# Attention outputs of tokens from 512 on: stored as two half-precision parts and turned by DMA transposes instead of by TensorE

## The chip, the cores and the metric

The kernel runs on one core of a Trainium2 chip. The time is in device microseconds (us) for one launch. A core has five engines with queues of their own, each working strictly in order: TensorE (PE in the profile, its weight loads PEld) for matmuls, VectorE (DVE) and ScalarE (ACT) for element-wise work, GpSimd (POOL) and SyncE (SP), which in this kernel mainly issue DMAs. An engine waits for another, or for a DMA, on semaphores.

## The reference

One decoder layer over 2048 tokens of width 1024. Two kinds of attention share one normalised input and one input projection; their outputs are gated, put side by side, sent through an output projection, normalised again and added to the input:

```python
oa = forgetting_attention(qa, ka, va, fa + b_fgate)      # 8 heads of 64, causal, decaying
oa = oa * silu(za)
ob = sliding_window_sink_attention(rope(qb), rope(kb), vb, sinks)   # 8 heads of 64, window 128
ob = ob * silu(zb)
y = concatenate([oa, ob], axis=-1) @ w_out
x = x + gate * rms_norm(y, g_post)
```

Everything is float32 in the reference. The kernel computes its large products with float32 numbers split into two float16 parts, high and low, and three matmuls per product (high by high, high by low, low by high).

## The kernel before, in words

The work goes in stages, all of it on one core, in an order that is written out by hand: the code lists small units of TensorE work, and a counter of ticks (`after(n, f)` puts work n ticks off, `tick()` runs what is due) decides when the VectorE and ScalarE work that belongs to a unit is put into the queues. Because queues are in order, the place at which a step is put in is also the place at which it can hold up what follows.

1. Input normalisation and the first projections. The gate inputs z, transposed (width in partitions, tokens along the free side), go to a DRAM tensor `z_d`.
2. Sliding-window attention (class `Pair`): 4 pairs of heads by 8 pairs of 128-query blocks, 32 windows, with projection units (L317, L335) put in between. The last step of a window (`out_`, L911 to L916) multiplies the PSUM result by 1/sum into a float32 tile `on` and GpSimd's queue stores it to the DRAM tensor `o_d`.
3. Forgetting attention (class `Step`): 8 heads, each with four chunks of 512 queries (`ci`) and 20 steps of two key blocks. A step takes scores (L1294 to L1297), exponentials (ScalarE, L1301), their split into parts (ScalarE L1305, VectorE L1308) and products with the values (L1318 to L1321). At the last step of a chunk the result is multiplied by 1/sum into `ona` (L1327), and SP stores it to `o_d` (L1328). Projections of later heads and the search for row maxima (L1245, L1248) stand between the steps. The queries, keys and extra rows of a head live in one of two large SBUF tensors, `Ts[0]` for even heads and `Ts[1]` for odd ones, each of four slots of 2048 half-precision columns.
4. Output (class `Out`), one object for each of 16 tiles of 128 tokens. `load` (L1398) brings the tile's row of `o_d` (tokens in partitions) and its gate z (width in partitions) into slots of `Ts[0]`, which is free since head 7 lives in `Ts[1]`. `turn` (L1406) transposes o with eight 128x128 float32 TensorE transposes into two PSUM banks (L1410). `gate` (L1416 to L1419) multiplies both banks with z on VectorE. `squares_` (ScalarE, L1423) sums squares, `scale_` adds them over partitions with a one-column matmul (L1427) and makes a power-of-two-like scale, and two more steps split the scaled product into high (ScalarE, L1437) and low (VectorE, L1438). `product` (L1489) multiplies with the output weights: 16 units per tile, each of three matmuls 128x512, in two halves of eight units; at the end of a half `evac` (L1498, L1499) reads the bank. `root` and `store` normalise, add x and write the result (L1518, L1519).

The units of stage 4 stand in a list `ounits`, about 16 per tile. The first 33 of them are spread over the last twelve steps of head 7; the others follow after the last step, two units to a tick. In this list, a tile's load stands two tiles ahead of its products, and its turn stands in the first half of the tile before it. Every SP transfer also waits for an older one: SP's DMAs share eight semaphores in turn.

Of the kernel before, what the change touches and what calls it, by code (L numbers as in the profile page):

```python
# [10 lines left out]
F32 = mybir.dt.float32  # L11
# [30 lines left out]
def hybrid_layer(  # L42
# [794 lines left out]
    class Pair:  # L837
# [62 lines left out]
        def pv(self):  # L900
            j, i = self.j, self.i
            po = ps_pv.tile([P, 4, 64], F32, tag="pv", name="pob")
            for e, (i_, k0, nk) in enumerate(self.blocks):
                for h in range(2):
                    for b in range(nk):
                        for n, (pp_, vv) in enumerate(((0, 0), (0, 1), (1, 0))):
                            PE.matmul(po[:, 2 * e + h, :], self.ptt[:, pp_, self.at[e] + h * nk + b, :],  # L907
                                      vb[:, k0 + b, self.g, 64 * vv:64 * vv + 64],
                                      start=(b == 0 and n == 0), stop=(b == nk - 1 and n == 2))

            def out_():  # L911
                on = onp.tile([P, 2, P], F32, tag="on", name="on")
                V.tensor_tensor(on[:].rearrange("p e (h d) -> p (e h) d", h=2), po[:],
                                self.rinv[:].unsqueeze(2).broadcast_to([P, 4, 64]), op=ALU.mult)
                G.dma_start(o_d[i // 4][(i % 4) * P:(i % 4 + 2) * P, (4 + j) * P:(5 + j) * P]
                            .rearrange("(e p) c -> p e c", p=P), on[:])  # L916

            after(1, out_)

# [356 lines left out]
    class Step:  # L1276
# [33 lines left out]
        def pv(self):  # L1310
            hd, ph = self.hd, self.ph
            if self.first:
                self.po_[0] = ps_po.tile([P, 4, 65], F32, tag="po", name="poa")
            po = self.po_[0]
            for n, (b, u0, o) in enumerate(self.blocks):
                for u in range(u0, 4):
                    pq = slice(o + (u - u0) * P, o + (u - u0 + 1) * P)
                    PE.matmul(po[:, u, :], ph[:, 0, pq], vt[:, b, hd, 0:65],  # L1318
                              start=(self.first and n == 0 and u == 0), stop=False)
                    PE.matmul(po[:, u, 0:64], ph[:, 0, pq], vt[:, b, hd, 65:VW], start=False, stop=False)  # L1320
                    PE.matmul(po[:, u, :], ph[:, 1, pq], vt[:, b, hd, 0:65], start=False,  # L1321
                              stop=(self.last and n == len(self.blocks) - 1))
            if self.last:
                rinv = sm(4, "a_ri")
                V.reciprocal(rinv[:], po[:, :, 64])
                on = op_.tile([P, 4, 64], F32, tag="ona", name="ona")
                V.tensor_tensor(on[:], po[:, :, 0:64], rinv[:].unsqueeze(2).broadcast_to([P, 4, 64]), op=ALU.mult)  # L1327
                SP.dma_start(o_d[self.ci][:, hd * 64:(hd + 1) * 64].rearrange("(u p) d -> p u d", p=P), on[:])  # L1328

        po_ = {}  # L1330

# [38 lines left out]
    w_raw = {}  # L1370

    def w_out_load(m):
        k, cc = m % KT, slice((m // KT) * CH, (m // KT + 1) * CH)
# [18 lines left out]
    class Out:  # L1392
# [5 lines left out]
        def load(self):  # L1398
            t = self.t
            rows_ = slice(t * P, (t + 1) * P)  # L1400
            self.o = Ts[0][:, t % 2, :].bitcast(F32)
            SP.dma_start(self.o, o_d[t // 4][(t % 4) * P:(t % 4 + 1) * P, :])
            self.z = Ts[0][:, 2 + t % 2, :].bitcast(F32).rearrange("p (k n) -> p k n", k=KT)
            SP.dma_start(self.z, z_d[:, :, rows_].rearrange("k p n -> p k n"))

        def turn(self, lag):  # L1406

            px = [bk[bank()][:].rearrange("p (k n) -> p k n", k=4) for _ in range(2)]
            for k in range(KT):
                PE.transpose(px[k // 4][:, k % 4, :], self.o[:, k * P:(k + 1) * P], ident[:])  # L1410
            self.hl = wpool.tile([P, 2, KT, P], F16, tag=("whl", "wraw")[self.t % 2], name="oz")
            self.sc = sm(1, "w_pw")
            hi, lo = self.hl[:, 0], self.hl[:, 1]
            gs = sm(1, "w_mx")

            def gate():  # L1416
                for h in range(2):
                    z = self.z[:, 4 * h:4 * h + 4, :]
                    V.tensor_tensor(z, px[h], z, op=ALU.mult)  # L1419

            def squares_():
                junk = stp.tile([P, KT, P], BF16, tag="st", name="zj")
                A.activation(junk[:], self.z, AF.Square, accum_out=gs[:])  # L1423

            def scale_():
                pg = bk[bank()][:, 0:1]
                PE.matmul(pg, ones[:], gs[:], start=True, stop=True)  # L1427
# [92 lines left out]

    outs = [Out(t) for t in range(NB)]

    ounits, oloads = [], {}
    for t, n in [(0, 0), (1, 0), (0, 1), (1, 1)] + [(t, n) for t in range(2, NB) for n in range(2)]:
        if n == 0 and t + 2 < NB:
            oloads[len(ounits)] = t + 2
        for q in range(KT):
            ounits.append(lambda t=t, n=n, q=q: outs[t].product(n, q))
            nxt = 2 if (t, n) == (0, 1) else t + 1 if n == 0 and 2 <= t < NB - 1 else None
            if q == 2 and nxt:  # L1530
                ounits.append(lambda nxt=nxt: outs[nxt].turn(4))
    opos = [0]
    N_IN = 4 * KT + 1

    def ofill(n, each=None):
        for _ in range(n):
            if opos[0] in oloads:
                outs[oloads[opos[0]]].load()
            ounits[opos[0]]()
            opos[0] += 1  # L1540
            if each:
                each()

    with tc.manual_schedule():
# [30 lines left out]
        for s, stp_ in enumerate(steps):  # L1575
# [43 lines left out]
            if not opened and pos[0] >= N_OPEN and (r >= 14 or not late):  # L1619
# [22 lines left out]
        tick()  # L1642
        tick()
        fxs.close()
        ofill(len(ounits) - opos[0], tick2)
        for _ in range(4):
            tick()

    foxo.close()
    fox.close()  # L1650
    bkx.close()
# [30 lines left out]
```

## Time and profile before

| what | value |
|---|---|
| median of 3 runs | 1189.14 us (1188.18 to 1190.87) |
| span of the profiled execution | 1188.7 us |
| what the page shows of that execution beside its span | nothing |
| instructions on TensorE, matmuls and weight loads each | 10853 |
| output transposes on TensorE (L1410) | 128, from 975.6 to 1161.8 us |
| last scores of head 7 | 1016.94 us |
| DRAM traffic | 71.04 MB read, 25.18 MB written |

In the profile a group's row reads: line, engine, operation, output and inputs by the program's names, shape, count, then busy time in us and mean duration in ns, then the idle time of the engine just before these instructions and what ended it. The chain is followed back from the last instruction, at each step to what released it. In the rows by stage, each engine's busy time is followed by its instruction count, in the order TensorE, its weight loads, VectorE, ScalarE, GpSimd; then come the granted TensorE clock, the share of time that the DMA engines are busy, and GB/s.

### The profile page before, as it was taken

The numbers are of one execution on the slowest core, as the hardware profiler recorded it, in microseconds if no ns is written. First come the engines' busy times: TensorE is split into PE (matmuls) and PEld (weight loads), VectorE is DVE, ScalarE is ACT, GpSimd is POOL, SyncE is SP. The second block draws the span as 40 slices with busy tenths as digits, with TensorE's granted clock in tenths as the row PEclk, the third lists the DMA queues.
The fourth block names the chain that finished last, engine by engine and source line by source line (L and its number), as shares of the span: only waits on it lengthen the run. The fifth ranks groups of instructions, "written<-read, shape, count | busy, mean of one in ns | idle before, by whom it ended". The sixth has DMA issues, their size and how long they took to land.

```text
span 1188.7 us, 27244 instructions
## 1 busy us (share of the span) xinstructions
PE 1147.3 (97%) x10853; PEld 693.6 (58%) x10853; DVE 914.1 (77%) x2263; ACT 665.9 (56%) x1102; POOL 115.2 (10%) x231
## 2 busy tenths in 40 slices
PE   5899999999999998999999999999999999999997
PEld 2475556765558976555555555555555555555554
DVE  7876678687776748688888889887888887766665
ACT  2784345464655521476766667666666778433332
POOL 2000112212121211001000101001000000000000
PEclk9899999999999999999999999999999999999999
DMA  9745433314223322413325322212311345455642
GB/s 333 277 121 87 84 89 99 61 59 109 83 70 88 58 63 63 65 50 95 68 70 72 102 63 60 50 48 71 48 42 39 92 127 176 147 171 184 198 167 96
DMA packets 87579, 120.22 MB, mean 101 GB/s; under 512 B 27508, under 2 KB 63388, under 8 KB 87452
## 3 DMA queue, kind: packets, MB, share of 16 engines
q1 hardware_dynamic: 76184, 85.69, 24.4%
q0 software_dynamic: 10832, 32.50, 13.2%
q8 instruction: 85, 1.39, 0.6%
q14 instruction: 42, 0.34, 0.1%
q10 hardware_dynamic: 436, 0.28, 0.1%
HBM read 71.04 MB, written 25.18 MB: 81 GB/s over the span
## 4 chain that ended last, share of the span: by engine, by line
PE 79%; DVE 10%; DMA 6%; issue 2%; ACT 2%; SPq 1%; DVEq 0%; ACTq 0%
PE bk L317 29%; PE bk L1489 13%; PE bk L335 7%; PE sta L1295 4%; PE sta L1294 4%; PE bk L1245 4%; PE poa L1320 2%; PE poa L1321 2%; PE poa L1318 2%; DMA wa<-in_w_ada_dram 2%; PE pxb L888 2%; PE pss L855 2%; PE pob L907 2%; DVE a_m L1248 1%; PE bk L1410 1%
## 5 line engine op out<-in xcount | busy, mean ns | idle before, releaser
L1301 ACT ACTIVATE p<-sta,lift,scl_qk 128x1024 f32<-128x1024 f32 (+2 forms) x160 | 172.0, 1075 | 143.7 <-PE sta L1295 88.2
L317 PE MATMUL bk<-hT,wh_qk 128*128 128x512 f16 x768 | 195.3, 380 | 0.0
L1248 DVE TENSOR_REDUCE a_m<-bk 128x1 f32<-128x512 f32 x192 | 130.5, 686 | 55.2 <-PE bk L1245 54.0
L1308 DVE TENSOR_TENSOR pha<-p,pha 128x1024 f16<-128x1024 f32 (+2 forms) x160 | 169.1, 1057 | 0.2 <-ACT pha L1305 0.2
L1489 PE MATMUL bk<-wohl,oz 128*128 128x512 f16 x744 | 167.0, 379 | 0.7 <-DVE oz L1438 0.7
L1305 ACT ACTIVATE pha<-p 128x1024 f16<-128x1024 f32 (+2 forms) x160 | 148.1, 926 | 5.4 <-PE poa L1321 0.7
L1489 PEld LDWEIGHTS <-oz 128*128 128x128 f16 x744 | 71.9, 99 | 79.4 <-DVE oz L1438 2.8
L317 PEld LDWEIGHTS <-wh_qk 128*128 128x128 f16 x768 | 72.5, 98 | 78.2 <-issue 6.6
L1321 PE MATMUL poa<-vt,pha 128*128 128x65 f16 x1088 | 116.1, 192 | 1.4 <-DVE pha L1308 1.2
L1318 PE MATMUL poa<-vt,pha 128*128 128x65 f16 x1088 | 116.5, 193 | 0.5 <-DVE ona L1327 0.4
L1320 PE MATMUL poa<-vt,pha 128*128 128x64 f16 x1088 | 116.5, 194 | 0.0
L1245 PE MATMUL bk<-T 66*128 66x512 f16 (+2 forms) x320 | 110.2, 350 | 3.1 <-DVE a_m L1248 3.0
L1294 PE MATMUL sta<-T 128*128 128x512 f16 (+1 forms) x320 | 110.9, 346 | 2.5 <-ACT p L1301 2.4
L1318 PEld LDWEIGHTS <-pha 128*128 128x128 f16 x1088 | 101.5, 96 | 15.1 <-DVE ona L1327 1.5
L1295 PE MATMUL sta<-T 69*128 69x512 f16 (+1 forms) x320 | 109.8, 348 | 0.0
L1320 PEld LDWEIGHTS <-pha 128*128 128x128 f16 x1088 | 100.9, 97 | 11.4
L1321 PEld LDWEIGHTS <-pha 128*128 128x128 f16 x1088 | 100.8, 99 | 1.8 <-DVE pha L1308 1.7
L317 PE MATMUL bk<-hT,wh_za 128*128 128x512 f16 x384 | 99.7, 378 | 0.0
L335 PE MATMUL bk<-wh_va,hT 128*128 128x128 f16 x1536 | 90.7, 219 | 0.0
L335 PEld LDWEIGHTS <-hT 128*128 128x128 f16 x1536 | 87.5, 98 | 4.7 <-issue 2.1
L317 PE MATMUL bk<-hT,wh_zb 128*128 128x512 f16 x384 | 88.9, 379 | 0.0
L317 PE MATMUL bk<-hT,wh_qb 128*128 128x512 f16 x384 | 87.4, 379 | 0.0
(498 smaller groups left out, 1860.4 us busy)
## 6 DMA issues: line engine op xcount, KB each, us to landing
hT<-in_x_dram SPq DMA_DIRECT2D x20, 512.0 KB
wa<-in_w_ada_dram SPq DMA_DIRECT2D x16, 512.0 KB
z_d<-tz POOLq DMA_DIRECT2D x32, 256.0 KB, 2.9
T<-stq SPq DMA_DIRECT2D x64, 128.0 KB
T<-o_d SPq DMA_DIRECT2D x16, 512.0 KB
T<-z_d SPq DMA_DIRECT2D x16, 512.0 KB
out_dram<-hT SPq DMA_DIRECT2D x15, 512.0 KB
xt<-in_x_dram SPq DMA_DIRECT2D x12, 512.0 KB
```

The lines of the kernel that those rows point to most:

```text
L317: PE.matmul(ps, whl[:, a, k, :], hT[ci][:, b, k, :], start=(k == 0 and n == 0), stop=(k == KT - 1 and n == 2))
L335: PE.matmul(ps[:, u * P:(u + 1) * P], hT[ci][:, a, k, u * P:(u + 1) * P], whl[:, b, k, :], start=(k == 0 and n == 0), stop=(k == KT - 1 an ...
L1245: PE.matmul(mx[:, :w], T[0:XM, 0, i * P:(i + 1) * P], T[0:XM, 2, pc * CH:pc * CH + w], start=True, stop=True)
L1294: PE.matmul(self.st[:, o:o + w], T[:, 3, kb_], T[:, 1, qc], start=True, stop=False)
L1295: PE.matmul(self.st[:, o:o + w], T[0:XR, 2, kb_], T[0:XR, 0, qc], start=False, stop=not diag)
L1301: A.activation(self.p32[:, :self.w], self.st[:, :self.w], AF.Exp, scale=scl[f"qk{self.hd}"][:], bias=lift[:])
L1305: A.activation(self.ph[:, 0, :self.w], self.p32[:, :self.w], AF.Copy)
L1308: V.tensor_tensor(self.ph[:, 1, :self.w], self.p32[:, :self.w], self.ph[:, 0, :self.w], op=ALU.subtract)
L1318: PE.matmul(po[:, u, :], ph[:, 0, pq], vt[:, b, hd, 0:65], start=(self.first and n == 0 and u == 0), stop=False)
L1320: PE.matmul(po[:, u, 0:64], ph[:, 0, pq], vt[:, b, hd, 65:VW], start=False, stop=False)
L1321: PE.matmul(po[:, u, :], ph[:, 1, pq], vt[:, b, hd, 0:65], start=False, stop=(self.last and n == len(self.blocks) - 1))
L1489: PE.matmul(py, self.hl[:, i, k, :], w_slot(8 * j + k)[:, cc], start=(k == 0 and m_ == 0), stop=(k == KT - 1 and m_ == 2))
```

## The change

Tokens 0 to 511 (tiles 0 to 3) stay as they were. For tokens from 512 on:

- `o_d` holds float16, two parts for each tile. At the end of a window or a chunk the float32 result is no longer stored directly: ScalarE copies it into the high part of a new tile `oh`, VectorE subtracts to get the low part a tick later, and then the same queue as before (GpSimd or SP) stores both parts with one DMA.
- `Out.load` has two DMA transposes, issued by SP, bring the high and the low part from DRAM into SBUF already turned.
- `Out.turn` has no TensorE transposes; `gate` adds both parts into a float32 tile `of` and multiplies that by z, both on VectorE.
- Loads stand four tiles ahead instead of two, in slots of both `Ts[0]` and `Ts[1]`. Tiles 4 and 5 use `Ts[1]`, and their loads are issued in the step before the last one, behind the last scores. Turns stand 22 units ahead of the tile's first product, with one tick more between the gate and the sum.
- A pool for `of` (two buffers of 4 KB per partition) takes the place of the exponentials' tiles, and the scratch for GpSimd's DMA descriptors is set to 8192 bytes per partition.

The diff, cut to its core:

```diff
-    o_d = [dram.tile([CH, D], F32, name=f"o_d{t}") for t in range(NCH)]
+    o_d = [dram.tile([CH, D], F32, name="o_d0")] + [dram.tile([4, 2, P, D], F16, name=f"o_d{t}") for t in range(1, NCH)]
...
+    def o_store(on, pool, ci, rows_, cols_, eng, lag):
+        if ci == 0:
+            eng.dma_start(o_d[0][rows_, cols_].rearrange("(u p) c -> p u c", p=P), on)
+            return
+        u0, u1 = rows_.start // P, rows_.stop // P
+        oh = pool.tile([P, u1 - u0, 2, on.shape[-1]], F16, tag="oh", name="oh")
+
+        def low():
+            V.tensor_tensor(oh[:, :, 1], on, oh[:, :, 0], op=ALU.subtract)
+            eng.dma_start(o_d[ci][u0:u1, :, :, cols_].rearrange("u n p c -> p (u n) c"),
+                          oh[:].rearrange("p u n c -> p (u n) c"))
+
+        after(lag, lambda: A.activation(oh[:, :, 0], on, AF.Copy))
+        after(lag + 1, low)
...
-                G.dma_start(o_d[i // 4][(i % 4) * P:(i % 4 + 2) * P, (4 + j) * P:(5 + j) * P]
-                            .rearrange("(e p) c -> p e c", p=P), on[:])
+                o_store(on[:], onp, i // 4, slice((i % 4) * P, (i % 4 + 2) * P), slice((4 + j) * P, (5 + j) * P), G, 1)
...
-                SP.dma_start(o_d[self.ci][:, hd * 64:(hd + 1) * 64].rearrange("(u p) d -> p u d", p=P), on[:])
+                o_store(on[:], op_, self.ci, slice(0, CH), slice(hd * 64, (hd + 1) * 64), SP, 1 if hd == 7 else 2)
...
         def load(self):
...
+            n = t % 2 if t < 4 or t % 4 > 1 else 2 + t % 2
+            T, n = Ts[n // 2], n % 2
...
+            if t < 4:
+                self.o = o.bitcast(F32)
+                SP.dma_start(self.o, o_d[0][rows_, :])
+            else:
+                self.oT = o.rearrange("p (l k n) -> p l k n", l=2, k=KT)
+                for n in range(2):
+                    SP.dma_start_transpose(self.oT[:, n], o_d[t // 4][t % 4, n])
...
             def gate():
-                for h in range(2):
-                    z = self.z[:, 4 * h:4 * h + 4, :]
-                    V.tensor_tensor(z, px[h], z, op=ALU.mult)
+                if self.t < 4:
...
+                of = ozp.tile([P, KT, P], F32, tag="of", name="of")
+                V.tensor_tensor(of[:], self.oT[:, 0], self.oT[:, 1], op=ALU.add)
+                V.tensor_tensor(self.z, of[:], self.z, op=ALU.mult)
...
-        if n == 0 and t + 2 < NB:
-            oloads[len(ounits)] = t + 2
...
+    for t in range(4, NB):
+        if t > 5:
+            oev.setdefault(start_[t - 4] + 1, []).append(outs[t].load)
+        oev.setdefault(start_[t] - 22, []).append(lambda t=t: outs[t].turn(5))
...
+            if s == len(steps) - 2:
+                outs[4].load()
+                outs[5].load()
...
+        ozp = ozx.enter_context(tc.tile_pool(name="ozp", bufs=2, side="right", reuse_waits="tile"))
...
-    nc = _bacc.Bacc("TRN2", target_bir_lowering=False, num_devices=1)
+    nc = _bacc.Bacc("TRN2", target_bir_lowering=False, num_devices=1, dynamic_dma_scratch_size=8192)
```

More of the change, by code (lines that the diff above doesn't have):

```diff
@@ L1368, in open_out @@
         V.tensor_scalar(wsc[:], fac8[:], ysc[:], None, op0=ALU.mult)
-    w_raw = {}
+    w_raw, ozp = {}, None
     def w_out_load(m):
@@ L1416, in gate @@
             def gate():
-                for h in range(2):
-                    z = self.z[:, 4 * h:4 * h + 4, :]
-                    V.tensor_tensor(z, px[h], z, op=ALU.mult)
+                if self.t < 4:
+                    for h in range(2):
+                        z = self.z[:, 4 * h:4 * h + 4, :]
+                        V.tensor_tensor(z, px[h], z, op=ALU.mult)
+                    return
+                of = ozp.tile([P, KT, P], F32, tag="of", name="of")
+                V.tensor_tensor(of[:], self.oT[:, 0], self.oT[:, 1], op=ALU.add)
+                V.tensor_tensor(self.z, of[:], self.z, op=ALU.mult)
             def squares_():
@@ L1521, in hybrid_layer @@
     outs = [Out(t) for t in range(NB)]
-    ounits, oloads = [], {}
+    ounits, oev, start_ = [], {}, {}
     for t, n in [(0, 0), (1, 0), (0, 1), (1, 1)] + [(t, n) for t in range(2, NB) for n in range(2)]:
-        if n == 0 and t + 2 < NB:
-            oloads[len(ounits)] = t + 2
+        start_.setdefault(t, len(ounits))
         for q in range(KT):
             ounits.append(lambda t=t, n=n, q=q: outs[t].product(n, q))
-            nxt = 2 if (t, n) == (0, 1) else t + 1 if n == 0 and 2 <= t < NB - 1 else None
+            nxt = {(0, 1): 2, (2, 0): 3}.get((t, n))
             if q == 2 and nxt:
                 ounits.append(lambda nxt=nxt: outs[nxt].turn(4))
+    N_IN = 4 * KT + 1
+    oev[0], oev[KT] = [outs[2].load], [outs[3].load]
+    for t in range(4, NB):
+        if t > 5:
+            oev.setdefault(start_[t - 4] + 1, []).append(outs[t].load)
+        oev.setdefault(start_[t] - 22, []).append(lambda t=t: outs[t].turn(5))
     opos = [0]
-    N_IN = 4 * KT + 1
     def ofill(n, each=None):
         for _ in range(n):
-            if opos[0] in oloads:
-                outs[oloads[opos[0]]].load()
+            for f in oev.pop(opos[0], []):
+                f()
             ounits[opos[0]]()
@@ L1647, in hybrid_layer @@
             tick()
+    ozx.close()
     foxo.close()
```

15 lines of the change are left out of this document (9 added, 6 removed).

## Prediction

> **What bounds the kernel now.** I read the page first (span, busy shares, shares of the chain), then busy time by stage, then the chain of waits inside the output stage, where the transposes stand.
>
> ```profile
> span 1188.7 us, 27244 instructions
> ...
> PE 1147.3 (97%) x10853; PEld 693.6 (58%) x10853; DVE 914.1 (77%) x2263; ACT 665.9 (56%) x1102; POOL 115.2 (10%) x231
> ...
> PE 79%; DVE 10%; DMA 6%; issue 2%; ACT 2%; SPq 1%; DVEq 0%; ACTq 0%
> ```
>
> TensorE is on the chain for 79% of the span and VectorE for 10%. By stage (sliding-window attention, the forgetting attention of heads 0 to 6 and part of 7, its last steps, the output products), with DVE and ACT as third and fourth pair of numbers:
>
> ```profile
> 150.00:435.00 285.00, 284.75 (x3330) 199.08 (x3329) 208.44 (x594) 152.27 (x418) 61.74 (x139) 1.00 0.33 78
> 480.00:975.00 495.00, 489.86 (x5020) 283.27 (x5019) 422.26 (x923) 334.12 (x391) 35.10 (x56) 1.00 0.30 66
> 975.00:1018.00 43.00, 41.57 (x448) 25.51 (x445) 32.55 (x57) 38.26 (x50) 0.54 (x1) 1.00 0.51 163
> 1018.00:1166.20 148.20, 147.59 (x800) 76.51 (x799) 97.57 (x275) 48.03 (x89) 0.00 (x0) 1.00 0.54 179
> ```
>
> VectorE is busy 73%, 85%, 76% and 66% of the four; ScalarE 53%, 67%, 89% and 32%. The granted clock (the 1.00) is full. TensorE's busy time has modelled ends, so the chain is the better witness:
>
> ```profile
> by line: PE bk L1489 89.8%; PE bk L1410 7.8%; PE bk L1427 0.9%; DVE hT L1498 0.5%; PE poa L1321 0.3%; DVE pha L1308 0.3%; PE poa L1318 0.2%; PE poa L1320 0.2%; issue 0.0%
> ```
>
> That is 1020 to 1166 us: almost nothing but TensorE, and its transposes (L1410) are 7.8%. A stretch of the same chain:
>
> ```profile
> 1065.80 4.53 PE bk L1489 x21
> 1070.33 0.87 PE bk L1410 x8
> 1071.20 3.88 PE bk L1489 x18
> 1075.09 0.12 PE bk L1427 x2
> ```
>
> Eight transposes are one tile's turn and cost 0.87 us with nothing beside them. A product matmul takes 4.53/21 = 0.216 us, a unit of three 0.65, a tile's 48 matmuls 10.4. With turn and sum a tile takes 11.4 us.
>
> **The change part by part.**
>
> *Removed: the turns of tiles 4 to 15.* By the instruction order this is the only thing that leaves TensorE: 12 x 8 transposes; twelve one-column sums (L1427) only move. 12 x 0.87 = **10.4 us off the path**, and a tile's period falls to 10.5 us. What is late next there is VectorE's gate, below.
>
> *Changed: the gate on VectorE.*
>
> ```profile
> L1419 DVE TENSOR_TENSOR T<-bk,T 128x512 f32<-128x512 f32 x32 | 20.6, 686 | 21.6 <-PE bk L1410 21.6
> ...
> L1308 DVE TENSOR_TENSOR pha<-p,pha 128x1024 f16<-128x1024 f32 x96 | 116.8, 1217 | 0.2 <-ACT pha L1305 0.2
> ...
> L1518 DVE SCALAR_TENSOR_TENSOR hT<-hT,y_rs 128x1024 f32<-128x1024 f32 x15 | 19.1, 1273 | 0.0
> ```
>
> Two multiplications of 0.69 us become an addition of the two parts and a multiplication over 1024 columns. The nearest rows say 1.22 and 1.27 us, so 2.5 instead of 1.4 per tile: +1.1. VectorE works 97.57/148.20 of the stage, 7.5 us a tile; with this 8.6 of 10.5. That is 82%, and TensorE's ten microseconds of products a tile hide it: nothing on the path. Were that cover gone, it would cost at most 12 x 1.1 = 13 us.
>
> *Added: 24 DMA transposes, 256 KB each, on SP's queue.* The trace of before has none, so the price is bounded by its transfers. One tile's 11.4 us in the output stage (the DMA view from 1086.5 to 1097.9), and from the page a transfer of the same size:
>
> ```profile
> q1 hardware_dynamic: 1472, 2.10, 55.8%
> ...
> T<-o_d SPq DMA_DIRECT2D x1, 512.0 KB
> ```
>
> ```profile
> z_d<-tz POOLq DMA_DIRECT2D x32, 256.0 KB, 2.9
> ```
>
> Four transfers of 512 KB fill the engines for 0.558 x 11.4 = 6.4 us. By bytes the load of o is a quarter of that, 1.6 us, and half of it, 0.8 us, is the low end for one transpose. The high end: each of its eight 128x128 blocks takes a whole landing like the 2.9 us, one after another, 23 us. I take 2.9 us, landing and all, from the row with the same bytes.
>
> How much may it cost? In the order, two transposes and a load of z for tile t are issued four tiles ahead, and the gate comes 22 units (14 us) before the tile's products. So latency is covered; rate is not. The other three transfers keep 6.4 - 1.6 = 4.8 us a tile, and of 10.5 us 5.7 are left: **2.85 us of engine time per transpose** is the point from which it would set the pace. A landing of 2.9 us has issue and flight in it, so its engine time is below that. Cost taken: nothing, narrowly.
>
> The start has its own deadline. The first transposes wait for the last scores, whose operands lie where they write:
>
> ```profile
> 1016.94 0.22 PE L1297 MATMUL sta<-dmaskT,identb 128*128 128x128 bf16 x1
> ...
> 1017.19 0.67 ACT L1301 ACTIVATE p<-sta,lift,scl_qk 128x384 f32<-128x384 f32 x1
> ```
>
> From about 1017 us. The products go on at about 1018 with unit 33; tile 4's turn is at unit 44 and its gate a tick later, 1018 + 13 x 0.65 = 1026.5. That is 9.5 us for two transposes and z; at 2.9 us each in a row, 8.7. VectorE now waits there for DMAs. Behind the waiting gate in its order stand the evacuations (L1498) that free TensorE's banks, and TensorE waits for those only when its five banks, each filled for 8 units or 5.2 us, are used up; and the low part of tile 4, planned for unit 58 and needed at 66, has 5.2 us of slack. So nothing is charged unless a transpose takes over some 4.5 us.
>
> *Added: 48 splits of attention outputs.* A ScalarE copy and a VectorE subtraction of 128x256, 24 in each attention.
>
> ```profile
> L1327 DVE TENSOR_TENSOR ona<-poa,a_ri 128x256 f32<-128x256 f32 x32 | 13.6, 424 | 1.1
> ...
> L1126 ACT ACTIVATE wsq<-wsq 128x256 f32<-128x256 f32 x31 | 12.5, 404 | 4.9 <-DMA wsq<-in_w_out_dram 4.9
> ```
>
> 0.42 us on VectorE, 0.40 on ScalarE: 20 us and 19 us of work. What of it reaches the path depends on whether VectorE is behind when it comes. Mostly it isn't; at a head's end it is:
>
> ```profile
> 619.49 0.23 PE bk L1245
> ...
> 619.74 0.69 DVE a_m L1248
> 620.43 1.19 DVE gacc L1182
> ...
> 623.73 0.70 DVE a_m L1248
> ...
> 624.47 0.27 PE bk L1245
> ```
>
> Here TensorE waits 4.7 us for a VectorE backlog, and anything added ahead of it adds its full length. The bounds are none (all in VectorE's idle time) and all of VectorE's 20 us. My choices: a tenth in the sliding-window stage, where VectorE idles 27% (24 x 0.42 x 0.1 = 1.0); a quarter in the 21 splits of heads 0 to 6, where it idles 15% (21 x 0.42 x 0.25 = 2.2); half of both engines' parts for the two splits from 975 to 1018, where ScalarE is 89% busy (2 x 0.82 x 0.5 = 0.8). The last falls after 1018 and costs nothing. Together **4.0 us**.
>
> *Moved: the stores.* They are issued two or three ticks later, from the same queues.
>
> ```profile
> SPq L1328 <- DVE ona L1327: 134.2, 27, 21.2
> ...
> POOL o_d L915 <- DVE on L913: 58.1, 21, 10.0
> ```
>
> Both queues already stand waiting for the store's data, so a later place in line costs them nothing; on SP the store lets short row loads (T<-rw) pass and, late, loads of weights and x; on POOL two small copies. The pieces get smaller (128 bytes on SP instead of 256), with the DMA engines at 0.30 busy. Nothing; a queue held 0.8 us longer before a q/k load (T<-stq) would be the loss, inside the upper bound above. The smaller descriptor scratch of POOL has no row here; its cover is POOL's 10%, and I charge nothing.
>
> *Sum.* The profiled execution's own time is its span of 1188.7 us; the page shows nothing around it. 1188.7 - 10.4 + 4.0 = 1182.3. The median of the runs, 1189.14, lies 0.4 above the span: **1182.7 us**.
>
> **The rivals.**
>
> *Transposes set the pace (slower).* The mechanism is the engines' time per tile: 4.8 + 2c against 10.5 us, for twelve tiles. It decides from c = 2.85 us. At 3.8 us: 12 x 1.9 = 23, so 1206. At 5 us: 52, so 1234. At the 23 us end: 12 x 40.3 = 484, so about 1670. For it: the price taken is close to the point, and no row shows a transfer that turns data. Against it: the row of 2.9 us is a landing, not occupancy; low end 0.8.
>
> [...]
>
> *The splits land where VectorE is behind.* If all of VectorE's 20.2 us reach the path: 1189.1 - 10.4 + 20.2 = 1198.9. The gain is gone at 10.4/20.2, about half. For it: 85% busy and backlogs like the one above. Against: three quarters of the chain is TensorE's.
>
> *The change doesn't do what it says.* The transposes leave, but TensorE stands for the same 0.87 us waiting for low parts, since VectorE's chain per tile got longer: 1189.1 + 4.0 = 1193.1. Against: 8.6 of 10.5 us.
>
> **How the numbers follow.** A run can tell about 0.2% (2.4 us) from no change. Forecast 0.64; transposes set the pace 0.22; splits 0.10; not what it says 0.04. The forecast's own range is 1178 (no cost of the splits, rounded down) to 1187. The range of 8 in 10 runs from 1177 to 1206: it takes in all of the splits' bound and transposes up to 3.8 us; the slower ones (0.16) and a time below (0.03) are left out. Faster by over 0.2% (below 1186.8): the forecast, 0.64. Within: part of the splits' case and of the last, 0.07. Slower: 0.29.
>
> **What would show it.** In the output stage the chain should be L1489's counterpart with no transposes and tile periods of 10.5 us; if transposes set the pace, the periods are uneven or longer, the DMA share is near 1 and VectorE's addition waits on DMA. The first gate should come near 1026 us less what came earlier. In 480 to 975 the stage should grow by about 2 us; 5 or more, and the splits were underpriced. Any wait of the addition on a transpose makes the prediction wrong.

## The result and the profile after

| | before | after |
|---|---|---|
| median (range, runs) | 1189.74 us (1188.18 to 1190.87, 4) | 1184.59 us (1183.7 to 1185.43, 4) |
| profiled execution | span 1188.7 | 1184.12 us, span 1182.4 |

The ratio is 0.9958, with a 95% interval of 0.9944 to 0.9972: faster by 0.42%, 5 us. A later, longer comparison of the same two kernels gave 0.9961 (0.9948 to 0.9973, 12 runs of the changed one). The forecast was 1182.7 us. In spans it was 1182.3, and 1182.4 was measured; that closeness hides errors that cancel, and the sections below take them apart.

The page of the changed kernel, busy times and shares of the chain:

```profile
PE 1136.7 (96%) x10757; PEld 682.6 (58%) x10757; DVE 941.3 (80%) x2311; ACT 680.9 (58%) x1150; POOL 116.1 (10%) x231
...
PE 80%; DVE 10%; DMA 5%; issue 2%; ACT 2%; SPq 1%; DVEq 0%; ACTq 0%
```

TensorE lost exactly 96 matmuls (12 tiles of 8 transposes) and 10.6 us of busy time. VectorE gained 27 us and ScalarE 15 us, and the shares of the chain are nearly unchanged.

To see where the 6.3 us of span went, a stage is best bounded by an operation that both kernels have. The view of one tile gives for each line its durations (min/median/max, ns) and the start of the first and the last of the count. Three such lines cut the span: the last step of a window (`on`), the last step of a chunk (`ona`), and the sum of squares that follows a tile's products (`y_ss`). Before:

```profile
L913 DVE TENSOR_TENSOR on<-pob,b_ri x32: 414/425/426, 165.2 to 433.2; 128x256 f32<-128x256 f32 x32
...
L1327 DVE TENSOR_TENSOR ona<-poa,a_ri x32: 424/424/426, 501.0 to 1023.2; 128x256 f32<-128x256 f32 x32
...
L1509 DVE TENSOR_TENSOR y_ss<-y_ss x15: 150/150/159, 1016.6 to 1172.4; 128x1 f32<-128x1 f32 x15
```

After:

```profile
L928 DVE TENSOR_TENSOR on<-pob,b_ri x32: 410/424/425, 165.4 to 436.4; 128x256 f32<-128x256 f32 x32
...
L1341 DVE TENSOR_TENSOR ona<-poa,a_ri x32: 423/424/426, 503.1 to 1026.5; 128x256 f32<-128x256 f32 x32
...
L1540 DVE TENSOR_TENSOR y_ss<-y_ss x15: 150/152/159, 1020.0 to 1165.8; 128x1 f32<-128x1 f32 x15
```

| stage | before | after | difference |
|---|---|---|---|
| to the first window's result | 165.2 | 165.4 | +0.2 |
| windows (sliding-window attention) | 268.0 | 271.0 | **+3.0** |
| last window to first chunk | 67.8 | 66.7 | -1.1 |
| chunks (heads 0 to 7) | 522.2 | 523.4 | **+1.2** |
| last chunk to first sum of squares | -6.6 | -6.5 | +0.1 |
| output, 14 tile periods | 155.8 | 145.8 | **-10.0** |
| last sum of squares to the end | 16.3 | 16.6 | +0.3 |

The differences add up to -6.3. So the gain is where it was forecast and nearly of the forecast size, and in this pair of profiles a loss of 3.4 us lies ahead of it. By an estimate that is some 1.7 us too little, because the granted clock of the two differed in the third stage of the table (0.91 before and 1.00 after from 470 to 490 us; e8 and e12, below).

The output stage by its chain, 1060 to 1095 us (start, length, what):

```profile
by line: PE bk L1520 99.5%; PE bk L1458 1.3%
...
1061.11 0.12 PE bk L1458 x2
1061.23 10.38 PE bk L1520 x48
1071.61 0.12 PE bk L1458 x2
```

Between a tile's two one-column sums (L1458) stand its 48 products without a break, and the period is 10.5 us; the 0.87 us of L1410 are gone and nothing has taken their place. The gate, by groups:

```profile
L1450 DVE TENSOR_TENSOR T<-of,T 128x1024 f32<-128x1024 f32 x12 | 14.7, 1224 | 0.4
L1449 DVE TENSOR_TENSOR of<-T 128x1024 f32<-128x1024 f16 x12 | 14.6, 1214 | 0.0
```

The addition (L1449) has no idle time before it: in twelve tiles VectorE never waited for a transpose. By stretches, from the start of tile 3's turn to the first product of the last half, first before and then after (TensorE, its loads, VectorE, ScalarE, GpSimd, clock, DMA share, GB/s):

```profile
1024.69:1175.74 151.05, 151.05 (x771) 77.17 (x770) 99.22 (x285) 49.34 (x91) 0.00 (x0) 1.00 0.55 182
```

```profile
1028.07:1169.15 141.08, 141.00 (x674) 66.16 (x673) 111.98 (x286) 49.99 (x91) 0.00 (x0) 1.00 0.68 184
```

VectorE's 12.8 us more lie under TensorE's products (111.98 of 141.08, 79%), and the DMA engines go from 0.55 to 0.68.

### The profile page after: what moved, and what is told of

It reads as the page before. It is cut to its first block, busy times and chain, and to the rows that moved or that the text cites. A ratio compares the mean times of both kernels' runs of the same rounds, so it can differ in the third digit from the quotient of the medians.

```text
span 1182.4 us, 27200 instructions
## 1 busy us (share of the span) xinstructions
PE 1136.7 (96%) x10757; PEld 682.6 (58%) x10757; DVE 941.3 (80%) x2311; ACT 680.9 (58%) x1150; POOL 116.1 (10%) x231
## 3 DMA queue, kind: packets, MB, share of 16 engines
q0 software_dynamic: 10832, 32.50, 13.5%
HBM read 64.75 MB, written 25.18 MB: 76 GB/s over the span
## 4 chain that ended last, share of the span: by engine, by line
PE 80%; DVE 10%; DMA 5%; issue 2%; ACT 2%; SPq 1%; DVEq 0%; ACTq 0%
PE bk L332 31%; PE bk L1520 13%; PE bk L350 7%; PE sta L1309 4%; PE sta L1308 4%; PE bk L1259 4%; PE poa L1334 3%; PE poa L1335 3%; PE poa L1332 3%; DMA wa<-in_w_ada_dram 2%; PE pxb L903 2%; PE pss L870 2%; PE pob L922 2%; DVE a_m L1262 1%; DVE pha L1322 1%
## 5 line engine op out<-in xcount | busy, mean ns | idle before, releaser
L1315 ACT ACTIVATE p<-sta,lift,scl_qk 128x1024 f32<-128x1024 f32 (+2 forms) x160 | 172.0, 1075 | 134.7 <-PE sta L1309 83.9
```

Source lines behind the costliest of these rows:

```text
L1315: A.activation(self.p32[:, :self.w], self.st[:, :self.w], AF.Exp, scale=scl[f"qk{self.hd}"][:], bias=lift[:])
```

## The experiments

The theory at this point: the gain is TensorE's own 12 x 0.87 us; transposes and gate are hidden; the splits cost the heads about 1 us and the windows something. The rivals: the gain comes from elsewhere (loads four tiles ahead, the order of turns); the transposes do cost; the loss in the windows is the splits', the stores', the scratch's, or mere scatter. Each kernel was timed beside the kernel before; the two profiles of one kernel can differ by some us of span (1182.4 and 1185.0 us for the change), so ratios decide on totals and the lines above on stages.

| kernel | median us (runs) | ratio to before [95%] | windows | chunks | output |
|---|---|---|---|---|---|
| before, first profile | 1189.74 (4) | | 268.0 | 522.2 | 155.8 |
| the change | 1184.59 (4) | 0.9958 [0.9944, 0.9972] | 271.0 | 523.4 | 145.8 |
| e1 splits only | 1192.09 (12) | 1.0023 [1.0014, 1.0033] | 270.4 | 523.5 | 156.0 |
| e2 plain copies | 1183.05 (6) | 0.9948 [0.9934, 0.9961] | 270.1 | 523.5 | 145.8 |
| e3 transposes twice | 1207.76 (4) | 1.0152 [1.0135, 1.0169] | 270.9 | 523.6 | 172.0 |
| e4 low part on GpSimd | 1182.86 (6) | 0.9945 [0.9932, 0.9957] | 269.8 | 522.8 | 146.0 |
| e5 no split | 1183.26 (6) | 0.9945 [0.9927, 0.9962] | 271.6 | 522.2 | 145.5 |
| e6 scratch only | 1189.5 (12) | 1.0001 [0.999, 1.0012] | 268.0 | 522.2 | 155.8 |
| e7 turn on TensorE again | 1215.97 (4) | 1.0223 [1.0204, 1.0243] | 270.3 | 523.5 | 177.7 |
| e8 the change again | 1184.34 (12) | 0.9961 [0.9948, 0.9973] | 272.0 | 523.5 | 145.8 |
| e9 idle transposes | 1194.43 (8) | 1.0042 [1.0027, 1.0057] | 269.9 | 523.5 | 156.0 |
| e10 high part only | 1182.95 (6) | 0.9942 [0.9923, 0.9961] | 269.1 | 522.4 | 145.6 |
| e11 split on GpSimd | 1183.21 (6) | 0.9944 [0.9927, 0.9961] | 270.1 | 523.5 | 145.7 |
| e12 before, second profile | 1190.39 (1) | | 268.0 | 522.2 | 155.7 |

The last three columns are worked out from the three lines as in the table above.

**e9: give TensorE its work back, and nothing else.** The change, with eight transposes per tile that nobody reads, at the turn's place:

```diff
+            else:
+                px = [bk[bank()][:].rearrange("p (k n) -> p k n", k=4) for _ in range(2)]
+                for k in range(KT):
+                    PE.transpose(px[k // 4][:, k % 4, :], gacc[:, k * P:(k + 1) * P], ident[:])
```

> The changed kernel with eight TensorE transposes per tile put back where the turn of tiles 4 to 15 stands, on data that has long been there (the gate weights); nobody reads their results. Theory (the gain of the change is TensorE's 12 x 0.87 us, nothing of it was or would be hidden): 10.4 us over the changed kernel, 1194.8, tile periods of 11.4 us. Rival (the output stage waits elsewhere too and hides part of them): 3 to 8 us over it.

Its sum of squares and its chain from 1060 to 1095 us:

```profile
L1544 DVE TENSOR_TENSOR y_ss<-y_ss x15: 150/153/159, 1023.4 to 1179.4; 128x1 f32<-128x1 f32 x15
```

```profile
1060.11 0.87 PE bk L1440 x8
1060.98 5.83 PE bk L1524 x27
1066.81 0.12 PE bk L1462 x2
1066.92 4.55 PE bk L1524 x21
1071.48 0.87 PE bk L1440 x8
```

The output stage takes 156.0 us, that of before, and the median rises to 1194.43, 9.8 above the changed kernel's first median and 10.1 above its second. With loads, order, DMA transposes and gate of the change all in place, the eight transposes alone carry the gain. It also prices the rest of the change: this kernel has all of it without the gain, and is 0.42% (0.27 to 0.57) above before, 5 us. So the result is -10 and +5.

**e2: transposes replaced by plain copies** (the turning is left out):

```diff
-                    SP.dma_start_transpose(self.oT[:, n], o_d[t // 4][t % 4, n])
+                    SP.dma_start(self.oT[:, n], o_d[t // 4][t % 4, n].rearrange("p (k n) -> p k n", k=KT))
```

> The changed kernel, with each DMA transpose replaced by a plain DMA copy of the same 256 KB into the same place, so that the output is computed from unturned data: the turning is left out. Theory (the transposes are hidden, deadline and rate both met): within 0.5 us of the changed kernel, 1184.6. Rival (transposes still cost something on the path, at the first tiles or by SP's time, whose issues of 1.2 to 3.4 us become some 0.4): 1 to 3 us faster, 1182 to 1183.5.

```profile
L1540 DVE TENSOR_TENSOR y_ss<-y_ss x15: 151/153/160, 1017.5 to 1163.3; 128x1 f32<-128x1 f32 x15
```

The output stage is 145.8 us, to the tenth that of the change: turning the data costs the path nothing. The median is 1.5 us lower, which is what the rival said. But the intervals overlap, and the profile has the difference in stages before the first transpose, where the two kernels are alike.

**e3: every transpose issued twice.**

```diff
-                for n in range(2):
+                for n in (0, 1, 0, 1):
```

> The changed kernel with every DMA transpose issued twice into the same place, 48 instead of 24, the result being the same. Theory by DMA engine time: the share of 67.5% in the changed kernel's output stage, less 4.8 us a tile for the other transfers, leaves 2.3 us for two transposes, so four make 4.8 + 4.6 = 9.4 us of a 10.5 us period: within 1 us of the changed kernel, 1184.6. Rival (SP's issue of a transpose, 1.24 to 3.4 us in the trace, is the real price): four issues of about 2 us and three others of 0.5 are 9.5 to 14 us a tile, so up to 12 x 3.5 = 42 us slower, 1190 to 1227.

The expectation that a second set would be hidden too fell: +23 us. The DMA engines from 1060 to 1150 us (packets, MB, share of the 16 engines), and SP's queue:

```profile
q1 hardware_dynamic: 39054, 19.04, 91.2%
...
T<-o_d SPq DMA_TRANSPOSE x29
```

```profile
1106.03 0.53 SPq L1429 DMA_DIRECT2D T<-z_d  x1
1106.61 0.57 SPq L1517 DMA_DIRECT2D hT<-in_x_dram  x1
1107.27 0.38 SPq L1550 DMA_DIRECT2D out_dram<-hT  x1
1107.75 10.06 SPq L1427 DMA_TRANSPOSE T<-o_d  x4
```

The same view of the DMA engines from 1060 to 1123 us, six tile periods, for the change and for e2:

```profile
q1 hardware_dynamic: 20640, 12.59, 74.7%
...
T<-o_d SPq DMA_TRANSPOSE x12
```

```profile
q1 hardware_dynamic: 9677, 12.55, 59.6%
...
T<-o_d SPq DMA_DIRECT2D x12, 256.0 KB
```

From these rows comes the number that the prediction had to bound. In the change the engines are busy for 0.747 x 63 = 47.1 us in six tile periods, 7.8 of each 10.5. Eighteen other transfers at 1.6 us each, by the prediction's row, leave 18.3 us for 12 transposes, 1.5 each. In e2, 0.596 x 63 = 37.5 us leave 8.7 for 12 copies, 0.7 each. These are estimates, since a transfer at a window's edge counts whole or not at all. The packets of the traces can be counted too: only the transposes move packets of 256 bytes, 1024 for each, and only e2's copies packets of 2048. In the same windows a transpose takes **1.4 us** of the engines by this count, a copy 0.7, and a transpose of e3 1.6.

In e3 four transposes at 1.6 and 4.8 us of other transfers are 11.2 us of engine time a tile, more than the 10.5 of the change's period. SP's queue is as full: 10.06 + 0.53 + 0.57 + 0.38 = 11.5 us for one tile's issues. Which of the two holds the stage up wasn't separated: an issue of a transpose took 1.2 to 4.7 us here, and how much of a long one is itself a wait for the engines isn't shown. But waits for DMAs are on the path: of the chain from 1040 to 1150 us, 21.4% are waits for the transposes and 20.3% for the stores of results.

The output stage grew by 26.2 us, and not all of that can be put down to the DMAs. The granted clock, 1.00 in the change from 1028 to 1169 us, was 0.5 in e3 for 27.2 us of the stage, in four stretches from 1038 to 1151 us. One of them, by stretch and in the chain:

```profile
1106.20:1113.00 6.80, 6.11 (x16) 2.52 (x17) 4.90 (x18) 2.45 (x5) 0.00 (x0) 0.50 0.96 270
```

```profile
1107.47 13.19 PE bk L1520 x48
```

Forty-eight products that take 10.38 us at the full clock took 13.19, 2.8 us more for the 5.5 us that they ran at half of it. Had TensorE set the pace in all 27.2 us, the clock would have cost 13.6, an estimate from above. So transposes can bring waits for DMAs onto the path, as the prediction's first rival says, and by engine time the change has a factor of two in hand at most (an estimate: 5.7 us a tile for transposes that take 2 x 1.4); how much of the 26.2 us is the transfers' and how much the clock's stays open.

**e7: the two parts loaded plainly, added on VectorE and turned on TensorE again**, a tick later:

```diff
+            if self.t >= 4:
+                of = ozp.tile([P, KT, P], F32, tag="of", name="of")
+                V.tensor_tensor(of[:], self.oT[:, 0], self.oT[:, 1], op=ALU.add)
...
-            if self.t < 4:
...
+            if self.t < 4:
+                flip()
+            else:
+                after(1, flip)
```

> The changed kernel with the turns of tiles 4 to 15 back on TensorE: both parts loaded by plain copies, added by VectorE, transposed by TensorE a tick later, the gate a tick after that. Theory (the gain is TensorE's 12 x 0.87 us and nothing else): 10.4 us over the changed kernel, 1195, tile periods of 11.4 us. Rival (TensorE had idle time that would have hidden part of the transposes, the gain is the earlier loads): at most 1190.

Measured 1215.97, far above that. Its chain from 1030 to 1150 us:

```profile
1048.62 1.23 DVE of L1435
1049.89 1.09 PE bk L1442 x8
1050.98 5.18 PE bk L1527 x24
1056.69 1.16 ACT oz L1475
...
1062.14 1.23 DVE of L1435
```

TensorE now waits in every tile for the addition, which stands in VectorE's queue, and once more behind 24 products for the scaled parts (`oz`); the period is 13.2 to 13.5 us. So this kernel put the transposes back along with waits of its own, and says little about them; e9 was made because of it. It does show what the cover of the gate is worth once TensorE needs VectorE's result a tick later instead of many units.

**e1: the splits alone.** The kernel before, with 48 splits computed and never stored, and the smaller scratch:

```diff
+    def o_split(on, pool, ci, n_u, lag):
+        if ci == 0:
+            return
+        oh = pool.tile([P, n_u, 2, on.shape[-1]], F16, tag="oh", name="oh")
+        after(lag, lambda: A.activation(oh[:, :, 0], on, AF.Copy))
+        after(lag + 1, lambda: V.tensor_tensor(oh[:, :, 1], on, oh[:, :, 0], op=ALU.subtract))
```

> The kernel before, with the 48 splits (ScalarE copy and VectorE subtraction of 128x256, at the ticks where the change has them) computed and thrown away; stores, loads and TensorE work are those of before, the descriptor scratch is 8192 bytes as in the change. In the changed kernel the turn of tile 3 starts 3.4 us later than before (1028.07 against 1024.69). Theory (the splits' engine time costs this): 3 to 4 us over before, about 1193. Rival (the later stores and their small pieces, or chance waits of TensorE, cost it): within 1 us of before, 1189.7.

```profile
L920 DVE TENSOR_TENSOR on<-pob,b_ri x32: 412/424/425, 164.5 to 434.9; 128x256 f32<-128x256 f32 x32
...
L1335 DVE TENSOR_TENSOR ona<-poa,a_ri x32: 423/424/426, 500.8 to 1024.3; 128x256 f32<-128x256 f32 x32
```

It is 0.23% slower, 2.7 us (1.7 to 3.9), which lies between the two expectations. In its profile the chunks take 523.5 us (+1.3, as in the change), and the windows 270.4 (+2.4).

**e5: no split.** VectorE writes its result in half precision at once, and the same tile is stored twice, as high and as low part (so the low part is left out and the high part counts double):

```diff
-                on = onp.tile([P, 2, P], F32, tag="on", name="on")
+                on = onp.tile([P, 2, P], F16 if i >= 4 else F32, tag="on" if i < 4 else "oh", name="on")
...
-                on = op_.tile([P, 4, 64], F32, tag="ona", name="ona")
+                on = op_.tile([P, 4, 64], F16 if self.ci else F32, tag="oh" if self.ci else "ona", name="ona")
```

> The changed kernel without the splits: VectorE writes the normalised output of tokens from 512 on directly in half precision, and two DMAs store that same tile as both parts, at the tick of the change; the low part is left out (the high part counts twice). Everything else is as in the change. Theory now (from the first four profiles, in which heads 0 to 7 lose 1.25 us between 500 and 1023 us and the sliding-window stage 0.2): 1.5 us faster than the changed kernel, about 1183. Rival (the 4.0 us of the prediction): 1180.6. Rival (the splits cost nothing, the losses are the stores'): 1184.6.

```profile
L924 DVE TENSOR_TENSOR on<-pob,b_ri x32: 412/424/426, 166.1 to 437.7; 128x256 f16<-128x256 f32 x24, 128x256 f32<-128x256 f32 x8
...
L1337 DVE TENSOR_TENSOR ona<-poa,a_ri x32: 423/424/425, 503.9 to 1026.1; 128x256 f16<-128x256 f32 x24, 128x256 f32<-128x256 f32 x8
```

Without splits the chunks take 522.2 us, what they took before. So the 1.2 us there are the splits'; with e1 that is shown from both sides. The windows are still 3.6 us longer, with no split in them.

**e10: high part only** (low parts left out: no split, one store and one transpose per tile, and a gate of one multiplication):

```diff
-                for n in range(2):
-                    SP.dma_start_transpose(self.oT[:, n], o_d[t // 4][t % 4, n])
+                SP.dma_start_transpose(self.oT[:, 0], o_d[t // 4][t % 4, 0])
...
-                of = ozp.tile([P, KT, P], F32, tag="of", name="of")
-                V.tensor_tensor(of[:], self.oT[:, 0], self.oT[:, 1], op=ALU.add)
-                V.tensor_tensor(self.z, of[:], self.z, op=ALU.mult)
+                V.tensor_tensor(self.z, self.oT[:, 0], self.z, op=ALU.mult)
```

> The low parts left out altogether: VectorE writes half precision directly, one part is stored, one transpose per tile instead of two, and the gate is one VectorE multiplication instead of an addition and a multiplication. Theory (second transpose and longer gate are hidden in the changed kernel): as the kernel without splits, 1183, that is 1 to 2 us under the changed kernel. Rival (the transposes or the gate still cost in the output stage): 1180 to 1181.5.

Half the transposes and half the gate give 145.6 us of output stage: a second sign that both are hidden. The windows still take 1.1 us more than before.

**e4 and e11: the split moved to GpSimd**, first the subtraction, then the copy too:

```diff
-            V.tensor_tensor(oh[:, :, 1], on, oh[:, :, 0], op=ALU.subtract)
+            G.tensor_tensor(oh[:, :, 1], on, oh[:, :, 0], op=ALU.subtract)
...
-        after(lag, lambda: A.activation(oh[:, :, 0], on, AF.Copy))
+        after(lag, lambda: G.tensor_copy(oh[:, :, 0], on))
```

> The changed kernel with the 48 subtractions for the low parts on GpSimd instead of VectorE; nothing else. Theory (the splits cost by VectorE's time): 20 us of VectorE work less, of which 10 to 15% reached the path: 1 to 3 us faster, 1182 to 1183.6. Rival (ScalarE's copies, the stores or chance waits cost it): within 0.7 us of the changed kernel; slower if GpSimd takes several us for one and its stores and loads of weights queue behind.

> The changed kernel with both halves of the split (copy to half precision and subtraction) on GpSimd; the values are the same. Theory (the splits cost by VectorE's and ScalarE's time in the attention stages, where GpSimd is 10% busy): at least what moving the subtraction alone gave, 1 to 2 us under the changed kernel, 1182.5. Rival (GpSimd's copies come late and hold up its own stores and weight loads, or share VectorE's way to memory): 1184.4 or over.

e4 saves 0.6 us of the 1.2 in the chunks (522.8), e11 nothing (523.5). So the heads' loss isn't the split's time on VectorE alone: e11 has none of the split there and the same loss. With the split on GpSimd, though, VectorE's own subtractions of 128x1024 (`pha`, 96 of them) took 1241 ns each in e4 and 1255 in e11, against 1216 in the change, which is 2.4 and 3.7 us in all; why isn't shown. Both medians are below the changed kernel's, by 1.7 and 1.4 us, and e2's, e5's and e10's by as much, but all their intervals overlap with 0.9944 to 0.9972. No version is shown to beat the change.

**e6: the kernel before with the smaller descriptor scratch**, `dynamic_dma_scratch_size=8192` and nothing else.

> The kernel before with GpSimd's descriptor scratch at 8192 bytes per partition as in the change, nothing else. In all five profiles with that scratch TensorE stands still once or twice for 0.9 to 1.8 us between 370 and 420 us, in the value products, waiting for nothing that the profile shows; the one profile of the kernel before has no such stop. Theory (the scratch brings the stops): one or two stops there, and 0 to 1.5 us over before, part of it given back at the wait for a DMA near 450 us. Rival (chance or the splits): no stop, 1189.7 as before.

No difference (1.0001), and the windows take 268.0 us. Its one profile had a span of 1185.3 us, 3.4 below that of before, at an equal median: a warning against reading a difference of few us from two spans. Of the 3.4, 2.1 lie between the last window and the first chunk (65.7 us against 67.8), which comes next.

**e8 and e12: the change and the kernel before once more**, without an edit, for a second profile of each.

> The changed kernel as it is, for comparison on the same chip and for a second profile. Expected: 1184.6, with one or two stops of TensorE near 375 and 407 us if they belong to the kernel, none if they are chance.

> The kernel before as it is, for a second profile. If the stops of TensorE between 370 and 420 us belong to the changed code, there is none here, as in the first profile and in the one with the smaller scratch alone; if they are chance, one may show.

The three stages repeat within 0.1 us, except for the windows of the change (271.0 and 272.0). So the windows' +3 isn't scatter: three profiles with the old instructions there (before, e6, e12) say 268.0, and eleven with new ones 269.1 to 272.0.

The stage from the last window to the first chunk does scatter, and the granted clock says why. From 470 to 490 us, first before and then after (the clock is the third number from the end):

```profile
470.00:490.00 20.00, 17.17 (x89) 8.05 (x86) 12.38 (x35) 5.21 (x9) 2.35 (x3) 0.91 0.15 38
```

```profile
470.00:490.00 20.00, 17.17 (x132) 9.93 (x131) 13.87 (x41) 4.62 (x8) 1.78 (x2) 1.00 0.15 38
```

Before ran at a granted clock of 0.50 from 475.3 to 478.7 us; an estimate from that is 3.4 x 0.5 = 1.7 us of work left undone. Sorted by this, the fourteen profiles fall into three groups: seven without such a stretch there take 65.7 to 67.1 us for this stage (the change: 66.7), six with one of 3.4 us take 67.3 to 69.0 (before: 67.8), and e9, with 6.8 us, takes 69.9. So the -1.1 of the table is no gain of the change. Without its stretch before would be at some 66.1, an estimate, and the row at +0.6; the loss ahead of the output stage is then 0.2 + 3.0 + 0.6 + 1.2 + 0.1 = 5.1 us, near the +5 of e9. With -10.0 and +0.3 that makes -4.6; the medians of the two comparisons differ by 5.2 and 4.4 (e8: 1184.34 against 1188.75). The 272.0 us of e8 have the same reason: behind a stop of TensorE (below) its clock was 0.5 from 377.7 to 381.1 us. What brings the half clock isn't shown.

**What lengthens the windows.** The chain of the changed kernel from 360 to 460 us, at the two places where the starts of its windows jump against those of before:

```profile
370.39 5.41 PE bk L350 x95
375.80 1.44 issue
377.24 0.89 PE bk L350 x13
...
407.79 1.12 issue
```

"Issue" is time in which TensorE waits for nothing that the profile shows: it stops in the middle of a dense row of 108 value-projection matmuls. The two stops are 2.6 of the 3.0 us. The chain of before has there

```profile
370.07 6.14 PE bk L335 x108
```

and no stop. Every kernel with changed instructions in the windows has one or two such stops, the longest of each 0.6 to 2.3 us, between 370 and 425 us: 1.07 and 0.97 in e1, 1.75 in e2, 1.57 and 0.88 in e3, 1.23 in e4, 0.61 and 1.15 in e5 (and 1.66 at 283.9), 1.70 and 0.31 in e7, 2.29 in e8, 1.69 in e9, 0.64 in e10, 1.17 and 0.30 in e11. Splits can't be what they have in common, since e5 and e10 have none; changed stores can't, since e1 has none; the scratch isn't the cause, by e6. The profile shows loads of instructions as DMA queues of their own (q8 and q14, 84 and 44 packets in the change), and none of these starts between 374 and 378 us or between 407 and 409 us in the change, so no such load is seen to end its stops. All these kernels issue other instructions than before in this stage, on engines other than TensorE. Why TensorE stops then stays open.

## Why the prediction was right, and where it wasn't

- **What bounds the kernel, and the term of -10.4.** Right: -10.0 in the output stage, and e9 shows that it is TensorE's time and all of it. Of the 0.4 us between, some 0.3 have a place in the change's chain: TensorE waited once for tile 3's low part, queued behind tile 4's longer gate on VectorE (30 products there took 6.89 us, 6.63 before); the rest was not followed.
- **The gate.** Right: 1.21 + 1.22 us against the 2.5 worked out, and VectorE at 8.3 of 10.5 us a tile against 8.6.
- **The transposes.** Right that they are hidden, and the price taken was too high: 2.9 us was a landing; the engine time is about 1.4. 4.8 + 2 x 1.4 = 7.6 of 10.5 us, where the prediction had only the decision point of 2.85. e3 then went past the point, with 4.8 + 4 x 1.6 = 11.2 above 10.5. The 1.4 us are for eight 128x128 blocks, 0.18 each, and the copies of e2 take 0.7 us of the engines where the transposes take 1.4, so the transposes ran at about half a copy's speed here.
- **The first deadline.** The first transposes did wait for the last scores, as said:

```profile
1007.64 14.11 SPq L1427 DMA_TRANSPOSE T<-o_d  x2
```

SP's queue stood at them from 1007.64 to 1021.75 us. But the first gate was forecast at 1026.5, 1029.9 with the 3.4 us by which all was late, and came at 1034.7. VectorE's timeline, in the change and in e2:

```profile
1026.55 0.42 DVE L1341 TENSOR_TENSOR ona<-poa,a_ri 128x256 f32<-128x256 f32 x1
...
1034.71 1.22 DVE L1449 TENSOR_TENSOR of<-T 128x1024 f32<-128x1024 f16 x1
```

```profile
1023.98 0.42 DVE L1341 TENSOR_TENSOR ona<-poa,a_ri 128x256 f32<-128x256 f32 x1
...
1032.15 1.21 DVE L1449 TENSOR_TENSOR of<-T 128x1024 f32<-128x1024 f16 x1
```

8.16 us after the last chunk's result in the one, 8.17 in the other, with transposes and with copies. So the transposes don't set it. The step that failed is the start of the count, 1018 us for unit 33. In the trace of before, the 99 products of the 33 units ahead of it run to 1023.2 (products up to 1023.3 us, their first and last start):

```profile
L1489 PE MATMUL bk<-wohl,oz x99: 376/379/390, 982.7 to 1023.2; 128*128 128x512 f16 x99
```

Counted from 1023.4, 13 units of 0.65 us and the 3.4 us give 1035.2, near the 1034.7 measured. The error only gave the transposes more room.

- **The splits, 4.0 us.** Mis-sized. In the heads 2.2 + 0.8 was charged, and 1.2 to 1.3 measured (e1, e5): that is an eighth of the 10.0 us that 24 splits took on VectorE, where a quarter was charged for heads 0 to 6 and half for the last. How the eighth reaches the path is open, since e11 loses as much with no split on VectorE. In the windows 1.0 was charged for VectorE's time; up to 368 us the changed kernel has +0.2 there. What the windows did lose, some 2.6 us of TensorE's stops, was in no term. The sum of what lies ahead of the output stage, 3.4 us (0.2 + 3.0 - 1.1 + 1.2 + 0.1), is near 4.0 by luck: a term too high stands in for one not foreseen, and the half clock of before hides 1.7 us. Without that it is 5.1.
- **Stores and scratch, nothing.** e6 shows it for the scratch. For the stores no run separates them from the stops.
- **From span to time, +0.4.** Wrong, and the larger part of the miss in the total. The prediction set the span of before, 1188.7, against the median of the runs. The profiled executions with a time of their own have 1184.12 - 1182.4 = 1.7 us (the change) and 1190.39 - 1188.6 = 1.8 us (before, second profile) around the span; in all thirteen it is 1.7 to 2.1. By that, the first profiled execution of before took about 1190.5 us, some 0.8 above the median, and the two errors nearly cancelled. For the changed kernel median and span are 2.2 apart (1.7, and an execution 0.5 under its median). 2.2 - 0.4 = 1.8 of the 1.9 us between 1182.7 and 1184.59 come from there.
- **The rivals.** Transposes set the pace: not here; with twice their number (e3), waits for transposes and for stores are 42% of the chain from 1040 to 1150 us. Splits where VectorE is behind: not at all of the size that decides, 1.2 us against 10. The change doesn't do what it says: no, by e9. The largest loss, the windows' 3 us, was in none of the three.

## What to carry to other kernels

Here, work taken off the engine that bounds a stage came back nearly in full (10.0 of 10.4 us), and it was worth transfers longer than the work removed (2 x 1.4 us of engine time a tile for 0.87 of TensorE) while DMA engine time per tile stayed under the period (7.6 of 10.5 us). Count both: with the transfers doubled (11.2 us), a gain of 5 us became a loss of 18, of which the clock may have a part. To undo one part of a change, add back the cost alone (e9: 156.0 us of output stage, as before), since a restored dependency (e7: 177.7) can bring a wait of its own. Where the difference is a fraction of a per cent, compare stages bounded by operations that both kernels have, not spans, look whether both ran at the same granted clock, and ask what lies around the span before a median is forecast from it.

## What the runs showed of the hardware

- A DMA transpose of 128x1024 half-precision numbers held its issuing queue for 1.49 us at the median, a copy of the same bytes for 0.43. First the change, then e2 (min/median/max in ns):

```profile
L1427 SPq DMA_TRANSPOSE T<-o_d x24: 1239/1486/3390, 1007.6 to 1124.9; - x24
```

```profile
L1427 SPq DMA_DIRECT2D T<-o_d x24: 326/433/982, 1005.1 to 1121.3; - x24
```

- The profile's count of bytes read from DRAM left these transposes out: 71.04 MB before, 64.75 after. The 6.29 MB between are 24 x 256 KiB, just what the transposes bring in.
- A subtraction of 128x256 in the heads took GpSimd 0.80 us (e4, 24 of them 19.3 us), against VectorE's 0.42.
- TensorE stopped for up to 2.3 us (e8) in a dense row of matmuls with nothing in the profile to wait for, between 370 and 425 us in every kernel with changed instructions in the windows, where only other engines' instructions had been changed.
- The granted clock fell to 0.5 for 3.4 us or 6.8 us in some executions and not in others of the same kernel (around 475 us: before and e8, not the first profile of the change). The stage took 1.9 us longer with a stretch of 3.4 us, by the means of the two groups.
